# The conditioning sums of a two-layer hybrid transformer kernel, all moved beside the attention heads, with a written order for TensorE

## The chip, the cores and the metric

The kernel runs on one core of a Trainium2 chip. The metric is the time of one execution on the device in microseconds (us). TensorE (PE) multiplies, VectorE (DVE), ScalarE (ACT) and GpSimd (POOL) do the elementwise work, and SyncE (SP) issues nearly all transfers from HBM.

## The reference, cut to what matters

One sequence of 512 tokens of width 1024 (and 256 context tokens) passes two layers. Layer 0 mixes with differential attention (6 heads, each with two score maps) and a Fourier branch, layer 1 with a short convolution. Each mixer is followed by a mixture of 16 experts. Six conditioning vectors per layer shift, scale and gate all this.

```python
sh_m, sc_m, g_m, sh_f, sc_f, g_f = split(silu(c) @ ada_w[l] + ada_b[l], 6)   # 1024 x 6144, each layer
s = einsum('bqhmd,bkhmd->bhmqk', q, k)                 # m = 0, 1; 512 queries, 768 keys
p = softmax(s)
a = p[:, :, 0] - lam * p[:, :, 1]
att = rmsnorm(einsum('bhqk,bkhe->bqhe', a, v), subln) * (1 - lam_init)
x = x + g_m * (concat(att, fourier) @ w_out)           # layer 0; in layer 1 the convolution
x = x + g_f * ec_moe(modulate(x, norm_ffn, sh_f, sc_f), ...)
```

## The kernel before, in words

The program is traced in Python. A scheduler then orders each engine's instructions by their place in the program (a smaller number goes first) as its own cost model finds them ready; on the chip each engine works through that fixed list and waits at semaphores. So an instruction whose input is late stops everything behind it on its engine.

The execution has four stages: attention (`attention`, to about 431 us in the profile), the experts of layer 0 (`moe`), the convolution (`conv`, about 915 to 1125 us), and the experts of layer 1.

Attention goes head by head, and each head in four steps `i` of 128 queries. While head `h` is attended to, the projections of head `H = h + 1` run as well: `proj` does one of six tiles of 128 tokens, 8 x 3 matmuls of 384 columns (256 for the two context tiles), because most operands are split into a high and a low part (`split`, `mm3`: three single-pass matmuls stand for one of full precision). `proj_fin` norms and rotates a tile on ACT, DVE and POOL, and `proj_tr` transposes two tiles of q and k. `scores` fills the PSUM tiles s0 and s1, `maxexp` takes the maxima on DVE and the exponentials on ACT, `normalise` combines the two maps, `att_tr` transposes the result in two groups of three, each into one of the two PSUM banks `tr` and out of it again, and `values` multiplies by v for two steps at once. `subnorm` and `subscale` norm what comes out. `fourier` runs behind heads 0 and 1. In the last head there is no projection left, and `wo.fill` begins the output projection.

The conditioning vectors are summed beside this by `ada_steps`: each is four parts of 1 MB (`ada_part`: a transfer, one ACT scaling, two DVE multiply-adds of 512 columns, and for all but the first part two POOL additions into `acc`, of which there is one buffer), and then `ada_sum` brings `acc` across the partitions on PE. Of the ten vectors that are not needed at once, seven are spread over 21 steps of the attention and three (`range(LW, 6)`, layer 1) over 11 steps of the convolution. Their parts share a ring of four 1 MB slots with the weights (wqk, wv, the Fourier matrix dft, later wo and cw); the transfers are issued in order by SP.

Line numbers in profiles: L68 is any `mm`, L251 and L250 the DVE and the ACT half of `split`, L174 and L176 the multiply-adds and additions of `ada_part`, L466 and L467 `maxexp`, L473 to L476 `normalise`, L489 `att_tr`, L443 `proj_tr`, L154 a load. Tiles: al and ah are the halves of the transposed attention, qv a head's values, ones<-ada the matmuls of `ada_sum` (an fp32 matmul of full precision is two instructions in the trace).

## Time and profile before

| | |
|---|---|
| time before, median of 3 runs | 1606.08 us (1604.41 to 1611.53) |
| the profiled execution | 1609.78 us, of which the span from first to last instruction is 1608.0 us |
| busy share of the span | PE 94%, DVE 42%, ACT 24%, POOL 14% |
| read from HBM | 491.41 MB |

A group of rows below is one view of this profiled execution. A busy PE includes the modelled tail of each matmul, so the distance from one start to the next is the better price of a matmul in a stream.

### The profile page before, as it was taken

The numbers are of one execution on the slowest core, as the hardware profiler recorded it, in microseconds if no ns is written. First come the engines' busy times: TensorE is split into PE (matmuls) and PEld (weight loads), VectorE is DVE, ScalarE is ACT, GpSimd is POOL, SyncE is SP. The second block draws the span as 40 slices with busy tenths as digits, with TensorE's granted clock in tenths as the row PEclk, the third lists the DMA queues.
The fourth block names the chain that finished last, engine by engine and source line by source line (L and its number), as shares of the span: only waits on it lengthen the run. The fifth ranks groups of instructions, "written<-read, shape, count | busy, mean of one in ns | idle before, by whom it ended". The sixth has DMA issues, their size and how long they took to land. (4 is left out here: it accounts for less than half of the span.)

```text
span 1608.0 us, 19864 instructions
## 1 busy us (share of the span) xinstructions
PE 1517.4 (94%) x7936; PEld 898.3 (56%) x7936; DVE 677.1 (42%) x1336; ACT 388.0 (24%) x753; POOL 225.3 (14%) x234
## 2 busy tenths in 40 slices
PE   4989999888999999999999899999899999999997
PEld 2978888777544444444443487887444444444443
DVE  3868788897612122112212567463312221221222
ACT  4535565553111001000100444232110010010000
POOL 0334355553000000000000024311000000000000
PEclk9889999999999999999999999999999999999999
DMA  9533444462799999999999766437999999999997
GB/s 346 168 103 106 156 136 155 158 236 104 302 364 360 410 409 409 409 409 409 409 409 404 265 209 209 157 131 271 348 399 399 409 409 409 410 408 409 409 409 278
DMA packets 162778, 494.79 MB, mean 308 GB/s; under 512 B 11750, under 2 KB 42879, under 8 KB 161663
## 3 DMA queue, kind: packets, MB, share of 16 engines
q1 hardware_dynamic: 161600, 491.23, 79.9%
q10 hardware_dynamic: 1086, 2.31, 0.4%
q8 instruction: 62, 1.02, 0.3%
q14 instruction: 30, 0.24, 0.0%
HBM read 491.41 MB, written 2.10 MB: 307 GB/s over the span
## 5 line engine op out<-in xcount | busy, mean ns | idle before, releaser
L1005 PE MATMUL s<-we,xs 128*64 128x512 f32 x1024 | 230.3, 597 | 0.0
L1005 PE MATMUL pj<-we,xs 128*64 128x512 f32 x1024 | 225.0, 593 | 4.5 <-DMA we<-in_moe_w_up_dram 4.5
L1005 PE MATMUL s<-we,aT 128*64 128x512 f32 x896 | 206.3, 603 | 0.0
L1005 PEld LDWEIGHTS pj<-we,xs 128*64 128x64 f32 x1024 | 75.6, 137 | 151.2 <-issue 140.8
L68 PEld LDWEIGHTS tr<-oh,x 128*128 128x128 f32 x1024 | 119.3, 191 | 50.2 <-issue 48.7
L1005 PEld LDWEIGHTS s<-we,xs 128*64 128x64 f32 x1024 | 69.3, 137 | 131.4 <-issue 125.8
L68 PE MATMUL tr<-oh,x 128*128 128x128 f32 x1024 | 131.2, 282 | 1.3 <-DVE oh L961 1.3
L1081 DVE TENSOR_TENSOR act<-act,pj 128x512 f32<-128x512 f32 x32 | 21.9, 688 | 261.3 <-PE pj L1005 240.3
L980 DVE TENSOR_SCALAR xs<-tr,am,ada 128x128 f32<-128x128 f32 x64 | 26.2, 409 | 230.4 <-PE tr L68 230.4
L1005 PEld LDWEIGHTS s<-we,aT 128*64 128x64 f32 x896 | 59.7, 137 | 103.2 <-issue 97.2
L1030 DVE TENSOR_TENSOR x<-x,tr 128x512 f32<-128x512 f32 x64 | 43.7, 685 | 139.8 <-PE tr L68 139.8
L176 POOL TENSOR_TENSOR ada<-ada,adaw 128x512 f32<-128x512 f32 x60 | 87.5, 1471 | 92.5 <-DVE adaw L174 45.4
L978 ACT ACTIVATE xs<-tr,ada,am 128x128 f32<-128x128 f32 x64 | 29.3, 458 | 273.2 <-DVE xs L980 273.2
L68 PE MATMUL pj<-whi,hh 128*128 128x384 f32 (+1 forms) x256 | 85.6, 334 | 0.3 <-ACT whi L250 0.3
L68 PE MATMUL pj<-wlo,hh 128*128 128x384 f32 (+1 forms) x256 | 83.1, 325 | 0.0
L68 PE MATMUL pj<-whi,hl 128*128 128x384 f32 (+1 forms) x256 | 83.0, 324 | 0.0
L1189 POOL TENSOR_TENSOR crs<-xsq 128x4 f32<-128x4 f32 x1 | 0.2, 203 | 485.2 <-ACT xT L1156 485.2
L1075 ACT ACTIVATE act<-s 128x512 f32<-128x512 f32 x32 | 17.4, 594 | 201.9 <-PE s L1005 168.3
L68 PE MATMUL pj<-chh,chi 128*128 128x512 f32 x160 | 62.4, 390 | 0.0
L68 PE MATMUL pj<-chl,chi 128*128 128x512 f32 x160 | 62.1, 389 | 0.0
L68 PE MATMUL pj<-chh,clo 128*128 128x512 f32 x160 | 62.0, 389 | 0.0
L710 POOL TENSOR_TENSOR wol<-wg,woh 128x512 fp32r<-128x512 f32 x32 | 47.2, 1489 | 96.6 <-ACT woh L709 91.7
(325 smaller groups left out, 2417.3 us busy)
## 6 DMA issues: line engine op xcount, KB each, us to landing
we<-in_moe_w_gate_dram SPq DMA_DIRECT2D x128, 1024.0 KB, 18.1
we<-in_moe_w_up_dram SPq DMA_DIRECT2D x128, 1024.0 KB, 18.2
we<-in_moe_w_down_dram SPq DMA_DIRECT2D x124, 1024.0 KB, 17.2
adaw<-in_ada_w_dram SPq DMA_DIRECT2D x48, 1024.0 KB, 5.6
cw<-in_conv_w_in_dram SPq DMA_DIRECT2D x12, 1024.0 KB, 6.4
wqk<-in_attn_w_in_dram SPq DMA_DIRECT2D x10, 512.0 KB
wo<-in_attn_w_out_dram SPq DMA_DIRECT2D x4, 1024.0 KB
we<-in_moe_w_down_dram SPq DMA_DIRECT2D x8, 512.0 KB
```

Source lines behind the costliest of these rows:

```text
L68: return T.matmul(o, l, r, start=start, stop=stop, skip_group_check=True)
L176: G.tensor_tensor(acc[:, cs], acc[:, cs], o, op=ALU.add)
L710: G.tensor_tensor(lo, wg, hi.bitcast(F32), op=ALU.subtract)
L978: A.activation(o_, i_, AF.Identity, bias=sh[:, kk:kk + 1], scale=am[:, kk:kk + 1])
L980: V.tensor_scalar(o_, i_, am[:, kk:kk + 1], sh[:, kk:kk + 1], op0=ALU.mult, op1=ALU.add)
L1005: pe(T.matmul(acc[hf][64 * j:64 * j + 64, :], lhs[:, 2 * kk + k, 64 * j:64 * j + 64], ws[j][:, k, hf * 512:hf * 512 + 512], start=kk == 0 ...
L1030: V.tensor_tensor(x1[tt][:, cs], src[tt][:, cs], b, op=ALU.add)
L1075: A.activation(act[:, hf * 512:hf * 512 + 512], ga[hf], AF.Silu)
L1081: V.tensor_tensor(act[:, cs], act[:, cs], up[hf], op=ALU.mult)
L1189: G.tensor_tensor(rs, xsq[:, :, 0], xsq[:, :, 1], op=ALU.add)
```

## The change: what it does

- `mm`, `turn` and the two matmuls of `subscale` are chained: in heads 0 to 4 each of them may be placed on PE only behind the one traced before it. The loop is rewritten: within a step come an even projection tile, `values` (now a step later), the next scores, `subnorm`, an odd projection tile, the rest of `fourier`, `subscale`, `proj_tr` and `att_tr`. `ada_sum`, the gate rows and the last head aren't in the chain.
- All ten vectors are summed in 20 steps of the attention, two parts a step; `conv` has none. `ada_sum` is traced at the start of the step behind a vector's last part, and is 4 packed matmuls of 256 columns, an ACT copy and 2 transposes in place of 8 matmuls of one column.
- v and the transposed attention are no longer split: `values` is 6 full-precision matmuls in place of 18 single-pass ones, and the ACT half of the split alone remains.
- `normalise` scales one map only (one ACT scaling of 768 columns less); the other map's sum goes into the epsilon of the norm behind it.
- A column is spread over a tile by one transpose (`spread`) in place of a matmul with the identity.
- The rotated sine table is half as large, and its multiplication is two DVE instructions in place of one.

```diff
+    def spread(o, col):
+        return T.transpose(o, col.to_broadcast([128, 128]), ident)
...
+    order = {"on": False, "last": None}
+    def inorder(m):
+        if order["on"]:
+            if order["last"] is not None:
+                tc.add_manual_dep(m.ins, order["last"].ins.name, NOSYNC, reason="the order of the heads")
+            order["last"] = m
+        return m
...
-        return T.matmul(o, l, r, start=start, stop=stop, skip_group_check=True)
+        return inorder(T.matmul(o, l, r, start=start, stop=stop, skip_group_check=True))
+    def turn(o, i):
+        return inorder(T.transpose(o, i, ident))
...
-        for k in range(KD):
-            mm(b[:, k:k + 1], acc[:, k * 128:k * 128 + 128], one1, True, True)
-        V.tensor_tensor(adaT[l, 0][:, w, :], b[:, :KD], biasT[:, l, w, :], op=ALU.add)
+        for q in range(4):
+            T.matmul(b[32 * q:32 * q + 32, 0:256], one1.to_broadcast([128, 32]), acc[:, 256 * q:256 * q + 256],
+                     start=True, stop=True, skip_group_check=True, tile_position=(0, 32 * q))
+        A.copy(acc[:, 0:256], b[:, 0:256])
+        for c in range(2):
+            T.transpose(b[:, 256 + c * 128:384 + c * 128], acc[:, c * 128:c * 128 + 128], ident)
+        V.tensor_tensor(adaT[l, 0][:, w, :].rearrange("p (q c) -> p c q", c=2),
+                        b[:, 256:512].rearrange("p (c q r) -> p c q r", c=2, q=4)[:, :, :, 0],
+                        biasT[:, l, w, :].rearrange("p (q c) -> p c q", c=2), op=ALU.add)
...
-            while n < len(todo) and n * steps < (step + 1) * len(todo):
+            if acc is not None and n % 4 == 0:
+                ada_sum(*todo[n - 1][:2], acc)
+                acc = None
+            while n < len(todo) and n * steps < (step + 1) * len(todo) and (acc is None or n % 4):
...
-                    if acc is not None:
-                        ada_sum(*todo[n - 2][:2], acc)
...
-                m = mm(b[:, k * 128:k * 128 + 128],
-                       adaT[l, 0][:, 2 + 3 * which, 4 * q + k:4 * q + k + 1].to_broadcast([128, 128]), ident,
-                       True, True)
+                m = spread(b[:, k * 128:k * 128 + 128], adaT[l, 0][:, 2 + 3 * which, 4 * q + k:4 * q + k + 1])
...
-        sing = tabs.tile([128, NT, 2, 2, 64], F32, name="sing")
+        sing = tabs.tile([128, NT, 2, 64], F32, name="sing")
...
-                for m in range(2):
-                    V.tensor_tensor(sing[:, :, j, m, :], sing[:, :, 1, 1, :],
-                                    gx_[:, j, None, :].to_broadcast([128, NT, 64]), op=ALU.mult)
+                for b in range(4):
+                    V.tensor_tensor(sing[:, :, j, 16 * b:16 * b + 16], sing[:, :, 1, 16 * b:16 * b + 16],
+                                    gj[:, None, 16 * (b ^ 1):16 * (b ^ 1) + 16].to_broadcast([128, NT, 16]),
+                                    op=ALU.mult)
...
-            a, b = [qkv.tile([128, 2048], F32R, tag="w", name=n) for n in ("qk", "qv")]
-            QKV[h] = ([a[:, 1536:], b[:, 1536:]], [a[:, :768], a[:, 768:1536]],
-                      [b[:, i:i + 768].rearrange("p (i d) -> p i d", i=6) for i in (0, 768)], {})
+            a = qkv.tile([128, 2048], F32R, tag="w", name="qk")
+            b = slot("qv", qkv)
+            ql = ap_.tile([128, S], F32R, tag="ql", name="ql", bufs=2)
+            QKV[h] = ([a[:, 1536:], ql], [a[:, :768], a[:, 768:1536]],
+                      b[:, :768].rearrange("p (i d) -> p i d", i=6), {})
...
-            split(v[0][:, tt, :], v[1][:, tt, :], p[:, 256:384])
+            A.copy(v[:, tt, :], p[:, 256:384])
...
-                src = p[:, :256].rearrange("p (g b i) -> p g b i", b=2, i=16)
-                V.tensor_tensor(t2.rearrange("p (g b i) -> p g b i", b=2, i=16), src[:, :, ::-1, :],
-                                sing[:, tt].rearrange("p j m (u b i) -> p (j m u) b i", u=2, b=2), op=ALU.mult)
+                for j in range(2):
+                    js = slice(128 * j, 128 * j + 128)
+                    V.tensor_tensor(t2[:, js].rearrange("p (m u b i) -> p m u b i", m=2, u=2, b=2),
+                                    p[:, js].rearrange("p (m u b i) -> p m u b i", m=2, u=2, b=2)[:, :, :, ::-1, :],
+                                    sing[:, tt, j, None, :].to_broadcast([128, 2, 64]).rearrange(
+                                        "p m (u b i) -> p m u b i", u=2, b=2), op=ALU.mult)
...
+        def normalise(i, p, su):
+
+            if i % 2 == 0:
+                AT["e"] = sm.tile([128, 2], F32, tag="e2", name="e2")
+            A.activation(AT["e"][:, i % 2:i % 2 + 1], su[:, 0:1], AF.Square, scale=EPS ** 0.5)
             rc = sm.tile([128, 2], F32, tag="rc", name="rc")
-            V.reciprocal(rc, su)
-            V.tensor_tensor(rc[:, 1:2], rc[:, 1:2], lam, op=ALU.mult)
-            A.activation(p[:, 1, :], p[:, 1, :], AF.Copy, scale=rc[:, 1:2])
-            V.scalar_tensor_tensor(p[:, 0, :], p[:, 0, :], rc[:, 0:1], p[:, 1, :], op0=ALU.mult,
-                                   op1=ALU.subtract)
-
-        AT = {}
+            V.reciprocal(rc[:, 0:1], su[:, 1:2])
+            V.scalar_tensor_tensor(rc[:, 1:2], su[:, 0:1], rc[:, 0:1], nlam, op0=ALU.mult, op1=ALU.mult)
+            V.scalar_tensor_tensor(p[:, 0, :], p[:, 1, :], rc[:, 1:2], p[:, 0, :], op0=ALU.mult, op1=ALU.add)
...
-                AT[0] = [ap_.tile([128, 6, 256], F32R, tag=f"a{x}", name=f"a{x}") for x in "hl"]
-            ah, al = AT[0]
+                AT[0] = ap_.tile([128, 6, 256], F32, tag="a" + "hl"[i // 2], name="at")
...
-                    T.transpose(b[:, c * 128:(c + 1) * 128], p[:, 0, (i0 + c) * 128:(i0 + c + 1) * 128],
-                                ident)
-                split(ah[:, i0:i0 + 3, qs], al[:, i0:i0 + 3, qs],
-                      b[:, :384].rearrange("p (i q) -> p i q", i=3))
...
+                    turn(b[:, c * 128:(c + 1) * 128], p[:, 0, (i0 + c) * 128:(i0 + c + 1) * 128])
+                A.copy(AT[0][:, i0:i0 + 3, qs], b[:, :384].rearrange("p (i q) -> p i q", i=3))
...
-                mm3(o[:, :256], (v[0][:, i, :], v[1][:, i, :]), (ah[:, i, :], al[:, i, :]), i == 0, i == 5)
+                mm(o[:, :256], v[:, i, :], a[:, i, :], i == 0, i == 5)
...
-            V.tensor_scalar(r, b[:, 256:258], 1.0 / 128, EPS, op0=ALU.mult, op1=ALU.add)
+            V.scalar_tensor_tensor(r, b[:, 256:258], 1.0 / 128, e2, op0=ALU.mult, op1=ALU.add)
...
-                mm(b[:, i * 128:i * 128 + 128], r[:, i:i + 1].to_broadcast([128, 128]), ident, True, True)
+                inorder(spread(b[:, i * 128:i * 128 + 128], r[:, i:i + 1]))
...
-            p = bank("pj", None)
-            for i in range(2):
-                mm(p, fh["bd"][i], fs[i], i == 0, i == 1)
-            V.tensor_copy(oT[:, 6 + g, :], p)
...
+            def rest():
+                p = bank("pj", None)
+                for i in range(2):
+                    mm(p, fh["bd"][i], fs[i], i == 0, i == 1)
+                V.tensor_copy(oT[:, 6 + g, :], p)
...
+            return rest
...
             H = h + 1 if h + 1 < NH else None
             for i in range(4):
                 p, su = maxexp(s)
+                if H and i < 3:
+                    proj(H, 2 * i)
+                if due:
+                    pend = values(*due)
+                    due = None
+                if i < 3:
+                    s = scores(h, i + 1)
+                normalise(i, p, su)
                 if pend:
                     pend = subnorm(*pend)
                 if H and i < 3:
-                    proj(H, 2 * i)
-                if i < 3:
-                    s = scores(h, i + 1)
-                normalise(p, su)
-                if H and 0 < i:
-                    proj_tr(H, i - 1)
+                    proj(H, 2 * i + 1)
+                if rest:
+                    rest = rest()
                 if pend:
                     subscale(*pend)
                     pend = None
+                if H and 0 < i:
+                    proj_tr(H, i - 1)
                 att_tr(h, i, p)
+                if i % 2:
+                    due = h, i // 2, AT[0], AT["e"]
                 if H and i == 3:
                     s = scores(H, 0)
-                if H and i < 3:
-                    proj(H, 2 * i + 1)
-                if i % 2:
-                    pend = values(h, i // 2)
                 if not H:
+                    if due:
+                        pend = values(*due)
+                        due = None
                     wo.fill(i, fold_router)
-                    fourier(h)
+                    rest = fourier(h)
...
-            mm(rb[:, tt * 128:tt * 128 + 128], rs[:, tt:tt + 1].to_broadcast([128, 128]), ident, True, True)
+            spread(rb[:, tt * 128:tt * 128 + 128], rs[:, tt:tt + 1])
...
-NSTEP = 21
-LW = 3
+NSTEP = 20
+LW = 6
```

## Rows read from the trace of the kernel before

**Rows 1.** The page's 40 slices (40.2 us each): granted PE clock in tenths, GB/s moved.

```profile
PEclk9889999999999999999999999999999999999999
GB/s 346 168 103 106 156 136 155 158 236 104 302 364 360 410 409 409 409 409 409 409 409 404 265 209 209 157 131 271 348 399 399 409 409 409 410 408 409 409 409 278
```

**Rows 2.** Windows, heads 0 to 5: length; busy PE, PEld, DVE, ACT, POOL; clock, DMA, GB/s.

```profile
93.03:135.42 42.39, 40.96 (x264) 35.92 (x265) 31.92 (x71) 24.68 (x57) 13.48 (x21) 0.97 0.15 51
135.42:187.35 51.93, 49.44 (x327) 43.47 (x327) 39.46 (x83) 25.85 (x54) 24.03 (x28) 0.97 0.39 126
187.35:240.13 52.78, 49.49 (x327) 43.75 (x327) 45.08 (x96) 33.60 (x70) 25.33 (x28) 0.97 0.52 176
240.13:287.96 47.83, 43.45 (x297) 37.86 (x296) 40.20 (x85) 27.63 (x61) 25.14 (x28) 1.00 0.40 132
287.96:342.36 54.40, 46.33 (x314) 41.12 (x312) 49.35 (x89) 30.18 (x61) 33.98 (x32) 0.94 0.63 218
342.36:389.43 47.07, 40.89 (x228) 33.41 (x228) 37.58 (x54) 19.76 (x37) 20.21 (x15) 0.96 0.37 134
```

**Rows 3.** PE's own waits from 90 to 395 us: total, times, longest.

```profile
PE tr L489 <- DVE p L476: 6.1, 6, 1.6
PE tr L68 <- DVE al L251: 5.8, 5, 3.3
```

**Rows 4.** Timeline of PE in head 0: start, us, what (x runs of one kind).

```profile
128.66 1.99 PE L68 MATMUL pj<-dft,oT 128*128 128x256 f32 x8
130.49 0.49 PE L489 MATMUL tr<-ident,p 128*128 128x128 f32 x3
...
135.21 0.39 PE L68 MATMUL tr<-ah,qv 128*128 128x256 f32 x1
...
137.42 1.02 PE L68 MATMUL pj<-four,bd_c 128*128 128x512 f32 x2
```

**Rows 5.** Timeline of PE beside the convolution, at two of the three sums.

```profile
965.42 1.84 PE L68 MATMUL tr<-ones,ada 128*128 128x1 f32 x16
967.12 0.48 PE L68 MATMUL pj<-chh,chi 128*128 128x512 f32 x1
...
992.25 2.79 PE L68 MATMUL tr<-ones,ada 128*128 128x1 f32 x16 [1.33 <-ACT gate L225]
```

**Rows 6.** Timeline of PE: four matmuls of 32 columns packed beside each other.

```profile
1119.71 0.85 PE L816 MATMUL tr<-xT,ra 128*32 128x384 f32 x8
1120.49 0.66 PE L831 MATMUL s<-ident,x 128*128 128x128 f32 x4
```

**Rows 7.** DVE groups, 93-342.4 us: count | busy, mean ns; L174's min/median/max ns, 90-400.

```profile
L174 DVE SCALAR_TENSOR_TENSOR adaw<-adaw,cin 128x512 f32<-128x512 f32 x35 | 30.3, 886 | 2.4 <-ACT adaw L170 2.4
L251 DVE TENSOR_TENSOR al<-tr,ah 128x384 fp32r<-128x384 f32 x40 | 21.7, 551 | 2.2 <-ACT ah L250 2.0
...
L251 DVE TENSOR_TENSOR qv<-pj,qv 128x128 fp32r<-128x128 f32 x30 | 8.4, 282 | 0.8 <-ACT qv L250 0.8
...
L174 DVE SCALAR_TENSOR_TENSOR adaw<-adaw,cin x39: 725/744/1796, 89.9 to 352.1; 128x512 f32<-128x512 f32 x39
```

**Rows 8.** Windows in and before the convolution (columns as in rows 2).

```profile
990.00:1000.00 10.00, 8.65 (x36) 6.88 (x35) 7.39 (x11) 7.04 (x12) 4.49 (x3) 0.66 0.72 219
1085.00:1100.00 15.00, 15.00 (x70) 12.93 (x69) 3.00 (x6) 0.62 (x1) 0.00 (x0) 0.77 0.67 237
```

**Rows 9.** Timeline of SP: start, us over which the loads were issued, count.

```profile
96.97 64.56 SPq L154 DMA_DIRECT2D adaw<-in_ada_w_dram  x6
...
273.53 34.30 SPq L154 DMA_DIRECT2D adaw<-in_ada_w_dram  x6
```

**Rows 10.** Timelines of PE and of DVE: the transposes of one `proj_tr`, the copy that ends it.

```profile
173.35 0.66 PE L443 MATMUL tr<-ident,qk 128*128 128x128 f32 x4
...
176.93 0.42 DVE L251 TENSOR_TENSOR qk<-tr,qk 128x256 fp32r<-128x256 f32 x1
```

**Rows 11.** Window just after the transposes that open the convolution (columns as in rows 2).

```profile
920.00:925.00 5.00, 5.00 (x13) 3.88 (x13) 5.00 (x9) 2.51 (x4) 0.00 (x0) 0.52 0.21 84
```

More of the change, by code (lines that the diff above doesn't have):

```diff
@@ L115, in body @@
     subg = cst.tile([128, 1], F32, name="subg")
-    lam = cst.tile([128, 1], F32, name="lam")
+    nlam = cst.tile([128, 1], F32, name="nlam")
     def small_loads(st):
@@ L144, in small_params @@
         A.activation(le, pl[:, 0:2], AF.Exp)
[L145 removed]
+        V.scalar_tensor_tensor(nlam, le[:, 1:2], LAM0, le[:, 0:1], op0=ALU.subtract, op1=ALU.subtract)
     def slot(name, pl=None):
@@ L201, in ada_steps @@
             yield
-        ada_sum(*todo[-1][:2], acc)
+        while n < len(todo) or acc is not None:
+            if acc is not None and n % 4 == 0:
+                ada_sum(*todo[n - 1][:2], acc)
+                acc = None
+                continue
+            l, w, j = todo[n]
+            n += 1
+            if j == 0:
+                acc = new()
+            ada_part((l, w, acc), j)
         yield
@@ L304, in attention @@
         cosg = tabs.tile([128, NT, 2, 64], F32, name="cosg")
-        sing = tabs.tile([128, NT, 2, 2, 64], F32, name="sing")
+        sing = tabs.tile([128, NT, 2, 64], F32, name="sing")
         gk1 = tabs.tile([128, 64], F32, name="gk1")
-        gx_ = tabs.tile([128, 2, 64], F32, name="gx")
         def table_loads(st):
@@ L321, in tables @@
             V.tensor_scalar(gb[:, 0, :], gb[:, 0, :], 0.125, None, op0=ALU.mult)
-            for b in range(4):
-                V.tensor_copy(gx_[:, :, 16 * b:16 * b + 16], gb[:, :, 16 * (b ^ 1):16 * (b ^ 1) + 16])
             for j in range(2):
@@ L442, in proj_tr @@
                     if j or g < 2:
-                        T.transpose(b[:, j * 256 + i * 128:j * 256 + i * 128 + 128],
-                                    nat[2 * g + i][:, j, :], ident)
+                        turn(b[:, j * 256 + i * 128:j * 256 + i * 128 + 128], nat[2 * g + i][:, j, :])
             cc = slice(g * 256, g * 256 + 256)
@@ L488, in att_tr, with values @@
                 for c in range(3):
-                    T.transpose(b[:, c * 128:(c + 1) * 128], p[:, 0, (i0 + c) * 128:(i0 + c + 1) * 128],
-                                ident)
-                split(ah[:, i0:i0 + 3, qs], al[:, i0:i0 + 3, qs],
-                      b[:, :384].rearrange("p (i q) -> p i q", i=3))
-        def values(h, qp):
+                    turn(b[:, c * 128:(c + 1) * 128], p[:, 0, (i0 + c) * 128:(i0 + c + 1) * 128])
+                A.copy(AT[0][:, i0:i0 + 3, qs], b[:, :384].rearrange("p (i q) -> p i q", i=3))
+        def values(h, qp, a, e2):
             v = QKV[h][2]
-            ah, al = AT[0]
             o = bank("tr", None)
             for i in range(6):
-                mm3(o[:, :256], (v[0][:, i, :], v[1][:, i, :]), (ah[:, i, :], al[:, i, :]), i == 0, i == 5)
+                mm(o[:, :256], v[:, i, :], a[:, i, :], i == 0, i == 5)
             sq = sm.tile([128, 256], F32, tag="osq", name="osq", bufs=1)
@@ L503, in values, with subnorm @@
             V.tensor_copy(at, o[:, :256])
-            return at, sq, h, qp
-        def subnorm(at, sq, h, qp):
+            return at, sq, e2, h, qp
+        def subnorm(at, sq, e2, h, qp):
             b = bank("tr", None)
@@ L619, in attention @@
                         NSTEP, lambda: sm.tile([128, D], F32, tag="ada", name="ada", bufs=1))
-        pend = None
-        wo = None
+        pend = due = rest = wo = None
         for h in range(NH):
             H = h + 1 if h + 1 < NH else None
+            order["on"] = H is not None
             if H:
@@ L895, in route @@
         bc = bank("tr", None)
-        n = spread(bc, isel, 0)[1]
+        n = tokens(bc, isel, 0)[1]
         gs = tmp.tile([NE, 2, CAP], F32, name="gs")
@@ L910, in route, with tokens @@
         return gf, bc
-    def spread(b, isel, e):
+    def tokens(b, isel, e):
         return [mm(b[:, j * CAP:j * CAP + CAP], ident[:NE, e + j:e + j + 1].to_broadcast([NE, 128]),
@@ L956, in onehot @@
                 b = bank("tr", None)
-                for m in spread(b, isel, e):
+                for m in tokens(b, isel, e):
                     pe(m)
```

5 lines of the change are left out of this document (2 added, 3 removed).

## The prediction

> **What bounds the kernel now.** I read the page's slices first. In both expert stages the transfers stand flat at about 409 GB/s, and they do so from the end of the stage before [rows 1]: those stages end a fixed time after their stream of weights can start. So a microsecond won in the attention or beside the convolution is won at the end, and one won among the experts is not. The change touches just those two stages, where the transfers run at a third to a half of that rate.
>
> Next, the attention head by head [rows 2]. Heads 0 to 4 take 249.3 us (93.0 to 342.4). PE is busy for 229.7 us of it, so it idles for 19.7. The granted clock falls short of full speed by 0.03, 0.03, 0.03, 0 and 0.06 of the five lengths: 7.8 us. What is left, about 222 us, is matmul work. DVE is busy for 206 us, 83%. PE sets the end, DVE is close behind, and the reader should see how little idle time there is to win. The waits say where it lies: PE stood about 1 us each time for DVE's combining of the maps or for DVE to empty a PSUM bank [rows 3]. Head 5 takes 47.1 us with 6.2 idle.
>
> Beside the convolution PE runs almost without a gap, so work taken off PE counts there in full. Three groups of one-column matmuls stand in it (two are shown, the third, at 1086, is like the first) [rows 5], and in the stretches around two of them the clock is at 0.66 and 0.77 [rows 8].
>
> **The change part by part: heads 0 to 4.**
>
> *Values.* Before, 18 single-pass matmuls in 137.42 - 135.21 = 2.21 us; full-precision matmuls of the same 256 columns start (130.49 - 128.66)/8 = 0.229 us apart [rows 4]. The new 12 instructions cost 2.75 us, 0.54 more. Nine pairs of steps fall into these heads: +4.9 us. What is saved is DVE's: the low halves al (21.7 us) and of v (8.4 us) [rows 7].
>
> *Sums.* One is 16 instructions in 967.12 - 965.42 = 1.70 us [rows 5]. The trace has no sum of the new kind. Eight packed instructions of 384 columns take 1120.49 - 1119.71 = 0.78 us [rows 6]; with 256 columns that bounds them from above if they run beside each other; one after the other, at 0.229, they would take 1.8. I take 0.78, since these too are 32 columns wide, plus 0.12 for two transposes (three of them fit into 0.33 us, 130.49 to the dft matmul after it, an estimate): 0.9. Six old sums save 0.8 each, three more come: -4.8 + 2.7 = -2.1 us (with 1.8: +6).
>
> *Spreading.* Each matmul with the identity is two instructions, each transpose one; at 1.70/16 = 0.106 us, nine times two in `subscale` and eight in the gate row save 26 x 0.106 = -2.8 us.
>
> So PE's own work stays as it is: 4.9 - 2.1 - 2.8 = 0.
>
> *Clock.* The dips stand behind stretches of many small matmuls. With the one-column groups gone I count half of the 7.8 us back: -4 (0 to -7.8).
>
> *The other engines.* DVE loses 30.1 us [rows 7]. The conditioning parts that run in these heads grow from 23 or 24 to some 37 of the 40, which is 27 more multiply-adds at 0.744: +20. The split rotation adds some 3, so DVE drops to about 199 us. ACT loses twenty scalings of 768 columns and gains thirteen of 1024 and ten small copies, near nothing; POOL gains some twenty additions. None becomes the bound of a stretch of 240 us; what hides them is PE's 222 us, and if a head were to fall under 40 us DVE would be next.
>
> *Idle time.* This is the real unknown. The written order gives each product a projection tile of PE work as cover: the maxima and exponentials of a step run under `proj`, the norm under the odd tile. But `subscale`, `proj_tr` and `att_tr` come in a row, with two `tr` banks for four users. The second group of `att_tr` can't begin before ACT and DVE have emptied the bank of `proj_tr`, and in a chain nothing else may fill the gap; before, the scheduler put projection matmuls there. Behind PE's instruction the whole chain queues, the next scores and maxima too. Fifteen steps of heads 0 to 4 have this. At best the copies take under a microsecond, mostly covered: 0.6 each, 9 in all. In the row nearest to it the transposes begin at 173.35 and the last copy ends at 177.35 [rows 10]; less the half microsecond that PE needs itself, 3.5 each, and 5 for the rest: 57. I take 1.2 each, by PE's present waits of about a microsecond for DVE [rows 3] since DVE has less to do: 18, which is -1.7 against 19.7.
>
> Heads 0 to 4: 0 - 4 - 1.7 = about -6 us.
>
> DVE's multiply-adds take 744 ns at the median and up to 1796, with a mean of 886 [rows 7]: some are held up. The Trainium skill (SBUF — State Buffer, section SBUF: two separate sides) says that a DVE instruction with two SBUF inputs and a GpSimd one that reads SBUF exclude each other for their whole length. By that rule, with which the spread agrees, some twenty more POOL additions would hold DVE up at just the steps where PE now waits for it, and with 0.6 us more a step the sum would end 9 us worse.
>
> **Head 5 and what follows.** DVE's low halves are gone there too. PE's longest single wait for one (3.3 us) was here [rows 3]; I count half of the 6.2 us of idle time: -3 (0 to -5).
>
> **Beside the convolution.** Three sums go: 1.70 twice and 2.7 us [rows 5], 6.1. Twelve spreads become transposes: 12 x 0.106 = 1.3. The clock costs 0.34 x 10 + 0.23 x 15 = 6.9 us in the two stretches [rows 8], about 1 of which is in the cold sum already. In both, two groups of small matmuls followed each other, and one of the two goes; behind the sum at 965.42 alone the clock stayed up. I count half of the rest: 3 (0 to 6). Twelve transfers of 1 MB leave the ring, and twelve parts leave ACT, DVE and POOL, where PE hides them anyway: nothing. Sum: -10.4 (-7 to -14).
>
> **The total.** -6 - 3 - 10.4 = -19.4 us. Made against the profiled execution, 1609.8, that gives 1590.4. That execution is 3.7 above the median of the runs, so the forecast for the median is 1606.1 - 19.4 = 1586.7: 1587 us.
>
> **The rivals.**
>
> *The heads close up.* The order does what it could: 9 us idle, the clock held (-4 more), the conditioning beside it hidden. Then -9 and -4 in the heads, -3 more beside the convolution: 1571 us. For it: every product has a tile of cover. Against: the bank argument above.
>
> *The chain is too strict.* The wait behind `proj_tr` is that of rows 10, so 57 us of idle time: +37 where I count -2, and the total is 1587 + 39 = 1626 us. It eats the whole gain once a step waits about 2.5 us, and shows as slower from about 3. For it: DVE is busy 83% of the time, and its list is in program order, so the rotation of the odd tile comes ahead of the copies. Against: 30 us of DVE work leaves exactly there.
>
> *The conditioning stream sets the end of attention.* In head 0 the ring is nearly blocked by weights and the Fourier matrix: six loads were issued over 64.6 us from 96.97 on; later six in 34.3, 5.7 us each [rows 9]. If twelve of the 40 parts are done when the second head ends, at about 187 us, the other 28 need 160 us, until 347, some 13 us behind the end of head 4 that I expect (93 + 243 = 336, less a little for the last sum). The output weights queue behind them on SP: 1600 us, no change worth the name. Against: PE, DVE and ACT waited little for these loads so far.
>
> *Transposes let the clock fall.* Ahead of the convolution, after a stretch of transposes and waits, PE ran at 0.52 for 5 us [rows 11], 2.4 us lost. The gate rows that come in the middle of each routing become transposes, eight in place of sixteen instructions, and the experts' first matmuls follow at once. Two such dips would give 5 us back: 1592 us. The Trainium skill (TensorE: Matmul & The Clock Gate, section Part 4: PE-mode transpose) states that transposes don't count as activity for the clock; the row agrees without proving it, as PE also waited there.
>
> **How the numbers follow.** Half a per cent (8 us, about what a measurement of this kernel can tell from no change) sets the bounds at 1598 and 1614. Forecast 0.46 (its own range 1576 to 1597), heads close up 0.17, transposes 0.08, stream 0.16 (0.03 of it faster), too strict 0.13 (0.02 of it within the bounds). Faster 0.74, same 0.15, slower 0.11. For eight in ten I go from the first rival's side, 1566, to just over no change, 1606.
>
> **What would show it.** Right: `values` at 12 instructions in about 2.7 us; sums of about 0.9 us on PE and none beside the convolution, with a full clock around 990 and 1090 of the old time; heads of 46 to 49 us; waits of about a microsecond behind `proj_tr`. Wrong: waits there of 2.5 us and more, or PE or DVE standing for conditioning loads; an expert stage that lengthens; or heads of 44 us.

## The result, and the profile after

The changed kernel takes 1622.32 us (median of six runs, 1614.96 to 1627.61) where the kernel before takes 1605.71: a ratio of 1.0103, 95% interval 1.0084 to 1.0123. It is slower by about 1%; the forecast was 1587, and the range ended at 1606. The profiled span grew from 1608.0 to 1625.8 us; the profiled execution of the changed kernel is the slowest of its six, some 5 us above the median.

By windows, heads 0 to 5 of the changed kernel (columns as in [rows 2]), then heads 0 to 4 as a whole, and head 5 with all that follows up to the routing (the choice of the experts):

```profile
90.56:132.90 42.34, 38.71 (x251) 33.54 (x251) 27.18 (x62) 19.52 (x52) 15.50 (x22) 0.94 0.22 73
132.90:195.54 62.64, 53.40 (x303) 44.62 (x303) 41.05 (x82) 28.50 (x64) 31.04 (x32) 0.88 0.39 135
195.54:257.67 62.13, 53.14 (x312) 44.95 (x313) 47.55 (x90) 32.78 (x74) 29.87 (x32) 0.93 0.58 193
257.67:314.04 56.37, 46.11 (x276) 38.82 (x275) 44.61 (x83) 28.98 (x65) 30.85 (x32) 0.88 0.49 169
314.04:371.83 57.79, 48.13 (x301) 40.98 (x300) 48.60 (x82) 31.67 (x65) 33.87 (x35) 0.94 0.71 245
371.83:417.52 45.69, 40.60 (x198) 31.26 (x198) 32.94 (x47) 17.23 (x37) 19.45 (x15) 0.89 0.46 160
...
90.56:371.83 281.27, 239.50 (x1438) 202.91 (x1438) 208.98 (x394) 141.46 (x320) 141.13 (x153) 0.91 0.49 168
371.83:464.30 92.47, 83.94 (x409) 62.76 (x410) 59.66 (x98) 29.92 (x64) 27.78 (x25) 0.91 0.51 184
```

The same last stretch in the kernel before:

```profile
342.36:431.00 88.64, 80.34 (x441) 62.10 (x442) 65.05 (x105) 31.51 (x61) 27.80 (x23) 0.98 0.48 177
```

Against [rows 2] the first head is as long as it was; the next four, in which the conditioning parts run, are longer. The five take 281.3 us in place of 249.3. PE idles for 41.8 us of that (19.7 before), and by the count used in the prediction (what the clock falls short of full speed, times the length) the clock costs 24.6 (7.7, where the prediction says 7.8). The two overlap, since the clock is low in part of the idle time too: 281.3 less both is 215, where the work is some 222. DVE was not relieved: 209 us busy, 206 before, 199 forecast.

Beside the convolution, from the first spread of its norm to the routing, the same view of the kernel before and of the changed one:

```profile
915.80:1126.90 211.10, 207.00 (x934) 167.57 (x934) 122.96 (x193) 72.30 (x117) 52.26 (x38) 0.95 0.56 194
```

```profile
952.10:1143.60 191.50, 190.14 (x874) 154.04 (x874) 101.29 (x165) 59.02 (x105) 23.95 (x20) 1.00 0.42 148
```

That is 19.6 us less, with a full clock to the end (0.66 and 0.77 in [rows 8]). So the balance of the span is -2.5 ahead of head 0 (90.56 for 93.03), +31.9 in heads 0 to 4, +3.8 from head 5 to the routing (92.5 for 88.6), +4.1 in the two expert stages (487.8 and 482.2 for 484.8 and 481.1) and -19.6 beside the convolution: together, but for rounding, the 17.8 seen.

The waits of PE, ACT and DVE from 90 to 345 us (total, times, longest), to be set beside [rows 3], which reach to 395 us:

```profile
PE tr L85 <- ACT at L525: 18.7, 13, 4.4
PE tr L69 <- POOL or L544: 4.5, 2, 2.9
PE tr L85 <- DVE oT L550: 3.1, 6, 1.8
...
ACT p L501 <- DVE nm L500: 32.6, 11, 5.1
ACT adaw L187 <- DMA adaw<-in_ada_w_dram: 19.4, 12, 5.0
...
DVE rc L513 <- ACT p L501: 19.9, 14, 3.6
```

PE stands before the second group of `att_tr` (L85) for ACT's copy (L525); ACT stands for the maxima of DVE. One such wait in the timelines of PE, ACT, DVE and POOL, in head 2:

```profile
231.83 0.60 PE L85 MATMUL tr<-ident,qk 128*128 128x128 f32 x4
232.26 0.49 PE L85 MATMUL tr<-ident,p 128*128 128x128 f32 x3
235.77 0.90 PE L85 MATMUL tr<-ident,p 128*128 128x128 f32 x3 [3.02 <-ACT at L525]
...
230.52 0.90 ACT L501 ACTIVATE p<-s,nm 128x768 f32<-128x768 f32 x1 [3.56 <-DVE nm L500]
...
234.21 1.15 ACT L187 ACTIVATE adaw<-adaw,cin 128x1024 f32<-128x1024 f32 x1
235.26 0.46 ACT L525 COPY at<-tr 128x384 f32<-128x384 f32 x1
...
224.63 3.48 DVE L191 SCALAR_TENSOR_TENSOR adaw<-adaw,cin 128x512 f32<-128x512 f32 x2
...
229.54 1.81 DVE L500 TENSOR_REDUCE nm<-s 128x1 f32<-128x768 f32 x2
...
236.24 0.41 DVE L283 TENSOR_TENSOR ql<-tr,qk 128x256 fp32r<-128x256 f32 x1
...
225.94 7.43 POOL L193 TENSOR_TENSOR ada<-ada,adaw 128x512 f32<-128x512 f32 x5
```

Read it from the bottom. POOL adds without a pause until 233.37 (the first of its additions, outside the row shown, starts at 224.28). The two multiply-adds on DVE that begin beside it at 224.63 take 3.48 us where two take 1.49 at the median of [rows 7]. Behind them in DVE's list stand a tile's rotation and then the maxima, which begin at 229.54; so the exponentials begin late, ACT's list slips by the same amount, with a conditioning scaling (L187) ahead of the copy, and PE, whose next instruction needs the bank, stands for 3 us. In all of heads 0 to 4 PE stood 26.2 us, in 19 waits, for this copy.

### The profile page after: what moved, and what is told of

It reads as the page before. It is cut to its first block, busy times and chain, and to the rows that moved or that the text cites. A ratio compares the mean times of both kernels' runs of the same rounds, so it can differ in the third digit from the quotient of the medians.

```text
span 1625.8 us, 19404 instructions
## 1 busy us (share of the span) xinstructions
PE 1514.7 (93%) x7744; PEld 888.2 (55%) x7744; DVE 654.1 (40%) x1276; ACT 373.4 (23%) x763; POOL 216.8 (13%) x234
## 4 chain that ended last, share of the span: by engine, by line
PE 78%; DVE 7%; DMA 5%; ACT 4%; POOL 2%; issue 2%; SPq 1%; DVEq 0%; ACTq 0%; POOLq 0%
PE s L1049 26%; PE pj L82 18%; PE tr L82 13%; PE pj L1049 12%; PE s L82 4%; DMA adaw<-in_ada_w_dram 3%; DMA we<-in_moe_w_down_dram 2%; PE pj L1151 1%; DVE adaw L191 1%; ACT p L501 1%; PE tr L85 1%; POOL ada L193 1%; DVE act L1125 1%; PE tr L1035 1%; ACT adaw L187 1%
## 5 line engine op out<-in xcount | busy, mean ns | idle before, releaser
L82 PEld LDWEIGHTS tr<-oh,x 128*128 128x128 f32 x1024 | 124.3, 199 | 50.2 <-issue 48.7
L82 PE MATMUL tr<-oh,x 128*128 128x128 f32 x1024 | 136.1, 289 | 1.3 <-DVE oh L1005 1.3
L82 PE MATMUL pj<-whi,hh 128*128 128x384 f32 (+1 forms) x256 | 89.4, 349 | 1.2 <-ACT whi L282 1.2
L754 POOL TENSOR_TENSOR wol<-wg,woh 128x512 fp32r<-128x512 f32 x32 | 43.1, 1361 | 179.5 <-ACT woh L753 179.5
L191 DVE SCALAR_TENSOR_TENSOR adaw<-adaw,cin 128x512 f32<-128x512 f32 x60 | 58.7, 1009 | 8.8 <-ACT adaw L187 8.8
```

The lines of the kernel that those rows point to most:

```text
L82: return inorder(T.matmul(o, l, r, start=start, stop=stop, skip_group_check=True))
L191: V.scalar_tensor_tensor(o, s[:, 0, cs], cin[:, 0, j:j + 1], s[:, 1, cs], op0=ALU.mult, op1=ALU.add)
L754: G.tensor_tensor(lo, wg, hi.bitcast(F32), op=ALU.subtract)
```

## The experiments

Each kernel was timed against the kernel before. "Heads" is the length of heads 0 to 4 and "DVE" its busy time in them, both by windows of the one profiled execution; time and ratio are those of the runs (the kernel before had medians of 1604.5 to 1606.2 in the sets). "chained" and "free" both mean the new parts in the new loop. e5 and e9 leave out the additions and e6 the scaling, so their conditioning sums are incomplete; they serve for the timing alone.

| kernel | vectors in attention | order | additions on | heads | DVE | time, us | ratio (95%) |
|---|---|---|---|---|---|---|---|
| before | 7 | old | POOL | 249.3 | 206.0 | 1605.7 | |
| changed | 10 | chained | POOL | 281.3 | 209.0 | 1622.3 | 1.0103 (1.0084-1.0123) |
| e1 | 10 | free | POOL | 249.7 | 204.3 | 1597.3 | 0.9961 (0.9934-0.9987) |
| e2 | 7 | chained | POOL | 251.6 | 182.7 | 1613.9 | 1.0064 (1.0039-1.0088) |
| e3 | 7 | free | POOL | 241.4 | 180.0 | 1600.6 | 0.9977 (0.9956-0.9998) |
| e4 | 10 | old, old parts | POOL | 275.6 | 226.2 | 1619.1 | 1.0092 (1.0062-1.0122) |
| e5 | 10 | chained | none | 249.5 | 185.0 | 1588.5 | 0.9888 (0.9866-0.9910) |
| e6, no ACT scaling | 10 | chained | POOL | 268.1 | 209.8 | 1607.8 | 1.0012 (0.9994-1.0030) |
| e7 | 10 | matmuls chained | POOL | 270.3 | 203.6 | 1611.9 | 1.0037 (1.0020-1.0054) |
| e8, gate by matmuls | 10 | free | POOL | 249.4 | 204.1 | 1594.3 | 0.9921 (0.9901-0.9940) |
| e9 | 10 | chained | fills on POOL | 258.6 | 183.9 | 1605.1 | 1.0004 (0.9988-1.0019) |
| e10 | 10 | free | DVE | 247.7 | 210.8 | 1593.9 | 0.9928 (0.9905-0.9952) |
| e11 | 10 | free | half each | 251.4 | 215.7 | 1596.5 | 0.9950 (0.9934-0.9966) |
| e12 | 10 | old, new parts | POOL | 262.7 | 213.3 | 1600.9 | 0.9965 (0.9949-0.9982) |
| e13 | 10 | chained | DVE | 261.7 | 215.8 | 1599.5 | 0.9967 (0.9946-0.9987) |
| e14 | 10 | old, old parts | DVE | 273.0 | 228.7 | 1626.4 | 1.0120 (1.0100-1.0140) |
| e15 | 7 | old, old parts | DVE | 244.0 | 209.5 | 1589.9 | 0.9889 (0.9869-0.9908) |
| e16 | 7 | free | DVE | 223.4 | 184.1 | 1577.4 | 0.9828 (0.9796-0.9860) |
| e17 | 8 | free | DVE | 232.4 | 193.1 | 1577.2 | 0.9822 (0.9790-0.9854) |
| e18 | 9 | free | DVE | 228.9 | 204.5 | 1571.2 | 0.9791 (0.9749-0.9832) |

### Chain or conditioning: e1 to e4

```diff
-            order["on"] = H is not None        # e1, e3
+            order["on"] = False
...
-NSTEP = 20                                     # e2, e3; e4 is the kernel before with 20 and 6
-LW = 6
+NSTEP = 21
+LW = 3
```

> The changed kernel with nothing chained: the new order of tracing stays, but the scheduler may place any matmul. Theory A (the chain is too strict: PE stands behind a transpose whose bank isn't empty yet): heads 0 to 4 fall from 281 to about 250 us, idle time of PE there from 42 to about 20, the whole about 1594 us (1588 to 1602). Theory B (thirteen more conditioning parts load DVE, ACT and POOL, and whoever sets PE's order waits for them): heads still 270 or more, the whole 1612 to 1624 us.

> The changed kernel with three vectors summed beside the convolution again, seven in 21 steps of the attention; the chain stays. Theory A: the heads hardly shorten (275 or more of 281 us) and the convolution is some 15 us longer, the whole 1630 to 1642 us. Theory B: heads of about 255 us, the convolution about 200, the whole 1604 to 1612 us.

> Both undone: nothing chained, three vectors beside the convolution; what is left are the new sums, values, norms and the new loop. Theory A: heads as without the chain alone, about 250 us or a little less, the whole 1600 to 1612. Theory B: heads about 250, as with the three vectors back alone, the whole 1600 to 1612; the two theories part at the two kernels with one of them undone.

> The kernel before with all ten vectors in 20 steps of the attention and none beside the convolution, in its own loop, with its own sums of eight one-column matmuls. Theory A: the heads take some 5 us more than before (255), the convolution some 15 us less, the whole about 1595 us (1588 to 1602). Theory B: the heads take 270 or more, the whole 1610 to 1622 us.

Heads 0 to 4 by windows, in e1, e2, e3 and e4:

```profile
90.97:340.70 249.73, 226.54 (x1435) 188.89 (x1436) 204.29 (x393) 139.52 (x320) 141.38 (x152) 0.99 0.54 187
```

```profile
90.42:341.99 251.57, 222.93 (x1409) 191.60 (x1409) 182.71 (x367) 130.13 (x308) 113.38 (x136) 0.97 0.41 142
```

```profile
90.51:331.89 241.38, 226.16 (x1404) 192.45 (x1405) 179.99 (x366) 129.29 (x307) 114.15 (x136) 0.95 0.43 146
```

```profile
89.87:365.51 275.64, 246.42 (x1553) 215.40 (x1553) 226.15 (x441) 151.23 (x307) 149.87 (x155) 0.92 0.52 179
```

Neither theory holds alone. e1 came as A said, with the heads at 249.7. But e2, with the chain in place, came as B said for the heads (251.6; its time, 1613.9, is 2 us above B's range), and e4, which has no chain at all, as B said too (275.6). In e3 the heads are shorter (241.4) than either had. The thirteen parts cost the heads 29.7 us where chained (281.3 - 251.6), 26.3 in the old loop (275.6 - 249.3) and 8.3 free (249.7 - 241.4); the chain costs 10.2 with seven vectors and 31.6 with ten. Each cost grows with the other. The reading that fits is that the chain makes PE wait for delays that the conditioning makes on other engines: e1 has the same parts, and DVE is nearly as busy (204 us), at heads of 249.7. The sizes are those of single executions, of the changed kernel its slowest and of e2 its fastest; by the medians the chain costs 13.3 us with seven vectors (1613.9 - 1600.6) and 25.0 with ten (1622.3 - 1597.3). The moved vectors also save more beside the convolution than was counted: in e4, with the old spreads, it takes 192.4 us where the kernel before takes 211.1.

### Which of a part's instructions: e5, e6, e9; where in the chain: e7

```diff
             if j:                                                            # e5: both lines go
-                G.tensor_tensor(acc[:, cs], acc[:, cs], o, op=ALU.add)
+                for _ in range(3):                                           # e9
+                    G.memset(o, 0.0)
...
-        A.activation(s[:, 1, :], s[:, 1, :], AF.Copy, scale=...)             # e6
...
-        return inorder(T.transpose(o, i, ident))                             # e7, subscale too
+        return T.transpose(o, i, ident)
```

> The changed kernel without GpSimd's additions of the conditioning parts (the later quarters of a vector are not added to the sum, so the conditioning is incomplete); loads, scalings and multiply-adds stay. Theory B1 (GpSimd's additions hold up VectorE's multiply-adds and all that is queued behind them): heads 0 to 4 fall from 281 to 265 us or less, and the mean multiply-add from 1032 to about 750 ns; the whole 1606 or less. Theory B2 (ScalarE's scalings, which stand waiting for their transfer in its queue, hold up the copies that PE waits for): heads 275 or more, the whole 1616 or more.

> The changed kernel without ScalarE's scaling in the conditioning parts (one half of each part goes unscaled into the sum); VectorE's multiply-add then waits for the transfer itself. Theory B2: PE's waits for ScalarE's copy of the transposed maps nearly vanish and heads 0 to 4 fall from 281 to 265 us or less, the whole 1606 or less. Theory B1: heads 275 or more, the whole 1616 or more. If each takes some 8 us, both engines count in the same chain.

> The changed kernel, chained, with each addition of GpSimd replaced by three fills of 512 columns of its own operand (the later quarters of a vector don't reach the sum): GpSimd waits for the same multiply-add, stays busy for about as long, but reads nothing from SBUF. Theory P (an addition and VectorE's multiply-adds shut each other out while both read SBUF): the multiply-add falls from 1032 to about 770 ns and heads 0 to 4 to about 252 us, as without additions; the whole 1588 to 1596. Theory Q (what hurts is GpSimd's queue: the norms' powers and the scaling of q and k stand behind the additions): heads 272 or more, the whole 1612 or more.

> The changed kernel with its transposes (projected tiles, combined maps, spread norms) out of the chain; the matmuls stay chained to one another, and all ten vectors stay in the attention. Theory A1 (PE stands because the next matmul may not pass a transpose that waits for its bank): heads 0 to 4 fall from 281 to about 253 us, as without any chain, the whole about 1600 (1594 to 1605). Theory A2 (the order of projection, values and scores among themselves binds): heads 270 or more, the whole 1612 or more.

Heads 0 to 4 by windows in e5 and in e9, then DVE's multiply-adds (count | busy, mean ns) in the changed kernel, in e5 and in e9, and their shortest, median and longest in the changed kernel and in e9:

```profile
85.65:335.12 249.47, 225.73 (x1431) 191.91 (x1432) 185.03 (x398) 142.62 (x323) 60.69 (x100) 0.95 0.58 199
```

```profile
88.75:347.31 258.56, 227.96 (x1433) 193.06 (x1434) 183.89 (x398) 141.95 (x322) 141.11 (x265) 0.95 0.55 190
```

```profile
L191 DVE SCALAR_TENSOR_TENSOR adaw<-adaw,cin 128x512 f32<-128x512 f32 x49 | 48.9, 1032 | 8.3 <-ACT adaw L187 8.3
```

```profile
L191 DVE SCALAR_TENSOR_TENSOR adaw<-adaw,cin 128x512 f32<-128x512 f32 x54 | 39.7, 766 | 15.8 <-ACT adaw L187 15.6
```

```profile
L191 DVE SCALAR_TENSOR_TENSOR adaw<-adaw,cin 128x512 f32<-128x512 f32 x54 | 39.2, 752 | 22.8 <-ACT adaw L187 22.7
```

```profile
L191 DVE SCALAR_TENSOR_TENSOR adaw<-adaw,cin x49: 734/747/1781, 89.2 to 342.1; 128x512 f32<-128x512 f32 x49
```

```profile
L191 DVE SCALAR_TENSOR_TENSOR adaw<-adaw,cin x54: 730/745/1101, 97.2 to 329.2; 128x512 f32<-128x512 f32 x54
```

Without POOL's additions the chained heads fall by the whole 31.8 us, although all loads, scalings, multiply-adds and sums are still there: B1. In e9 POOL is busy for the same 141 us, now with fills; the multiply-add is at 752 ns all the same, and the heads give back 22.7 us. So what slows the multiply-adds is not that POOL works, but that it reads SBUF beside them. The mean hides how: of the 72 multiply-adds in heads 0 to 4 of the changed kernel 13 took 1.75 to 1.78 us, about a microsecond more than the median, and most of the rest nothing more. The medians divide it more evenly: from 1622 to 1605 with fills and on to 1588 without them, so some 17 us each, and P's ranges for the heads (252) and the time (1588 to 1596) were missed. The second half, which fills cost too, I can't place: e9's profiled execution was its fastest, and the waits of e5 and e9 show no row of that size. Theory P for the larger part by the profile and for half by the medians, then, with a remainder that Q may own.

ACT's scalings cost 13.2 us in the same chain (e6, 268.1), which fits their place ahead of the copies; the bound of 265 for B2 was just missed. And e7, at 270.3 us and 1611.9, stands at the bounds of A2 (270 and 1612): that the matmuls are chained to each other costs more than that the transposes are, though with free transposes a third of the chain's cost goes.

### The gate rows: e8

e1, with `spread` in `gate_row` replaced by the matmul with the identity of the kernel before.

> The kernel without the chain, with the gate rows spread by matmuls with the identity as in the kernel before, in place of transposes. Theory G (after transposes alone the clock falls: 0.66 over 10 us in the second routing): the clock behind the gate rows stays at 1.0 there, each expert stage ends 1 to 2 us earlier, the whole 2 to 4 us below the kernel without the chain (1597), that is 1593 to 1595. Theory H (the dip comes from the waits of that stretch, or the stream of weights covers it): the same time within 1 us, with the same dip in the first case.

The second routing in the timeline of PE, the gate row and the experts' gathers behind it, and the window around the gathers: the kernel before, then e8.

```profile
1135.10 2.02 PE L68 MATMUL tr<-ident,ada 128*128 128x128 f32 x16 [0.45 <-DVE tv L876]
...
1141.06 4.03 PE L68 MATMUL tr<-oh,x 128*128 128x128 f32 x32 [0.67 <-DVE oh L961]
```

```profile
1141.90:1146.90 5.00, 5.00 (x38) 3.71 (x38) 1.18 (x3) 0.92 (x2) 0.00 (x0) 1.00 0.67 261
```

```profile
1121.38 2.02 PE L82 MATMUL tr<-ident,ada 128*128 128x128 f32 x16 [0.46 <-DVE tv L922]
...
1127.33 6.75 PE L82 MATMUL tr<-oh,x 128*128 128x128 f32 x32 [0.67 <-DVE oh L1007]
```

```profile
1128.20:1133.20 5.00, 5.00 (x25) 5.00 (x25) 0.74 (x2) 0.46 (x1) 0.00 (x0) 0.50 0.65 260
```

The same instructions with the same waits ran at full clock in one kernel and at 0.50, which is the lower level, in the other. So the dip doesn't need the gate row's transposes, as H said; but the waits, to which H put it, don't account for it either, as the kernel before has them without the dip. (The run's median, 1594.3, is G's time, 3 us below e1's; but they were timed in different sets, the intervals of the ratios overlap, and e8's profiled span is the longer one.)

### Additions on DVE: e10, e11, e13 to e15; the old loop: e12

```diff
-                G.tensor_tensor(acc[:, cs], acc[:, cs], o, op=ALU.add)
+                V.tensor_tensor(acc[:, cs], acc[:, cs], o, op=ALU.add)       # e11: for one of two
```

e10 and e11 are e1 with this, e13 the changed kernel, e14 is e4, e15 the kernel before. e12 is e1 with the order of the old loop.

> The kernel without the chain, with all additions of the conditioning parts on VectorE in place of GpSimd. Some 56 additions more on VectorE at some 0.6 us (an estimate from its multiply-adds of the same size) are 33 us, against 13 us that its multiply-adds save when GpSimd is silent. Theory P: VectorE 204 + 20 = 224 us of 250, heads unchanged within 4 us of 250, the whole 1594 to 1602. Theory R (VectorE's own load is what binds): heads 258 or more, the whole 1604 or more.

> The kernel without the chain, with one of each two additions on VectorE, the other on GpSimd. Theory P: half of the exclusion goes for some 17 us more on VectorE: heads 244 to 250, the whole 1590 to 1598. Theory R: heads 253 or more, the whole 1600 or more.

> The changed kernel's parts (unsplit values, packed sums, the shorter norm, all ten vectors in the attention), nothing chained, in the loop order of the kernel before. Theory S (the new loop, with values a step later, makes the stream of conditioning cheap where the old loop pays 26 us for it): heads 265 or more, the whole 1608 or more. Theory T (the new parts make it cheap, above all less work on VectorE): heads about 250 as in the new loop without the chain, the whole 1593 to 1601.

> The changed kernel, chained, with all additions of the conditioning parts on VectorE, none on GpSimd; nothing is left out. VectorE gets some 56 additions at 0.685 us (38 us) and its multiply-adds fall from 1032 to about 750 ns (-14). Theory P (what the chain stands behind is the trouble that GpSimd's additions make: exclusion and GpSimd's queue): heads 0 to 4 fall from 281 to 262 us or less, the whole 1594 to 1605. Theory R (in a chain any more work on VectorE or ScalarE ahead of the copies is paid): VectorE at 233 us and more, heads 272 or more, the whole 1613 or more.

> The kernel before with all ten vectors in the attention, in its own loop, and the additions on VectorE. With the additions on GpSimd its heads took 275.6 us, with VectorE busy for 226. Theory P: heads 264 or less, the whole 1608 or less, though VectorE rises to about 245. Theory R (VectorE is the engine that binds in the old loop with ten vectors): heads 275 or more, the whole 1617 or more.

> The kernel before, with seven vectors in the attention and three beside the convolution, with all additions on VectorE. Theory P: with fewer parts there is less trouble to remove, heads 244 to 250 of 249 us, the whole 1598 to 1605. Theory R: VectorE goes from 206 to about 228 us of 249, heads 255 or more, the whole 1610 or more.

Heads 0 to 4 in e13, and DVE's groups:

```profile
85.12:346.85 261.73, 232.22 (x1427) 194.81 (x1426) 215.79 (x455) 142.44 (x322) 64.46 (x99) 0.92 0.53 184
```

```profile
L191 DVE SCALAR_TENSOR_TENSOR adaw<-adaw,cin 128x512 f32<-128x512 f32 x54 | 39.6, 764 | 7.1 <-ACT adaw L187 7.1
L193 DVE TENSOR_TENSOR ada<-ada,adaw 128x512 f32<-128x512 f32 x55 | 35.8, 683 | 0.0
```

e13 is the changed kernel with nothing left out and 36 us of additions put onto DVE. DVE's busy time rises by only 7, the heads fall by 19.6 us, and 1622 becomes 1599: theory P for the chain. The kernel before gains 1.1% by the same line alone (e15), more than P had. The heads are not all of it: of e15's 16.6 us of span 5.4 lie in them, 7.1 ahead of head 0 (which begins at 86.0 in place of 93.0) and 5.9 beside the convolution. But in the old loop with ten vectors the line gains nothing (e14, 1626.4 us; e4 took 1619.1, with intervals that overlap): DVE is busy for 229 of 273 us there, the low halves of v and of the maps among it, and head 5 with what follows takes 105.6 us as against 92.5 in e4. The time is R's; the heads, at 273.0, lie between P and R, just below R's bound. e10 came as P said, but its time isn't clear of e1's; e11, with half of the additions moved, has P's time and heads no shorter than with none or all (251.4), which neither theory had. e12 has heads between S and T and the upper end of T's time: of the 26 us of heads between e4 and e1 the new parts are worth 13 (275.6 to 262.7) and the new order, unchained, the other 13.

### How many vectors: e16 to e18

e10 with `LW` of 3, 4 and 5 (`NSTEP` 21, 21 and 20).

> The changed kernel's parts without the chain, additions on VectorE, three vectors beside the convolution and seven in 21 steps of the attention. Theory P (with GpSimd silent a part costs the heads little, so the move pays what the convolution saves, 14 to 18 us for three vectors): the convolution about 205 us, attention some 10 us shorter than with all ten (347), the whole 1596 to 1602, above the 1594 with all ten. Theory R (VectorE's load is what the last three vectors cost): the attention 15 us or more shorter, the whole 1582 to 1592.

> The same with two vectors beside the convolution, eight in 21 steps of the attention. Theory P: between 1594 and 1600 us, each vector moved saves about 2 us. Theory R: 1585 to 1592, below the kernel with all ten, since attention shortens by more than the 5 us that a vector costs beside the convolution.

> The same with one vector beside the convolution, nine in 20 steps of the attention. Theory P: about 1595 us. Theory R: 1588 to 1592 us.

Heads 0 to 4 in e16, in e18, and in e10:

```profile
84.44:307.87 223.43, 216.61 (x1398) 184.75 (x1398) 184.05 (x401) 127.00 (x306) 62.69 (x99) 0.99 0.45 156
```

```profile
85.04:313.89 228.85, 219.37 (x1418) 185.29 (x1418) 204.51 (x436) 135.53 (x317) 65.17 (x99) 0.99 0.55 190
```

```profile
85.86:333.60 247.74, 233.13 (x1420) 193.98 (x1420) 210.84 (x449) 139.22 (x318) 64.20 (x99) 0.95 0.55 192
```

All three lie below the times of both theories. R had the direction, but that DVE's load is what the last vectors cost isn't shown: each vector takes ACT's scalings, the sums on PE and 4 MB of transfers with it. With no additions on POOL the heads are at 223 to 232 us, 17 to 26 below the kernel before. Nine vectors are the best that was run: 1571 us, 2.1% faster than the kernel before, with the convolution at 193.2. e18's interval overlaps those of e16 and e17, so only the step to ten vectors, which lengthens the heads by 19 us, is plain. Why the tenth costs so much wasn't tried; DVE's share doesn't tell, as it was busy for 89% of e18's heads and 85% of e10's.

## Why the prediction was wrong

**The other engines: the step that failed.** Twenty-seven more multiply-adds on DVE and some twenty more additions on POOL (25 and 18 by the traces) were costed at nothing, hidden by PE's 222 us, because no engine's busy time reached the length of the heads. With the scalings, sums and transfers of their parts they cost 26 us in the old loop (e4) and 30 in the chain. The error was to ask whether an engine has time left over, where what counts is how late each result comes that PE waits for next: DVE and ACT work through lists, and 3.5 us of held-up multiply-adds hold back the maxima, the exponentials and the copies behind them.

**The exclusion was seen and priced too low.** The prediction weighed what the Trainium skill (SBUF — State Buffer, section SBUF: two separate sides) states, that a DVE instruction with two SBUF inputs and a GpSimd one that reads SBUF exclude each other for their whole length, and said that the sum would end 9 us worse by it. By that rule fills, which read nothing, should leave the multiply-adds alone, and the trace agrees: 752 ns with fills and 766 without additions, against 1032. To take the additions off POOL gave 20 (e13) to 32 us (e5) of heads, POOL's queue included, and fills in their place 23 (e9). The bare delay of these multiply-adds is 49 x (1032 - 766) ns = 13 us; other DVE instructions were held as well, as all of DVE's busy time falls by 24 us in e5 (209.0 to 185.0) and 25 in e9. How much of the price is this delay itself and how much what stood behind it isn't shown.

**Idle time** was taken at 18 us and measured 41.8; the long waits are at the place named, ahead of the second group of `att_tr`, 3 us and more in the worst case. But the prediction had PE wait there for the bank of `proj_tr`; in the row shown the wait ends with the copy of the first group, while DVE still reads `proj_tr`'s bank at 236.24. **The clock** was to give 4 us back, as dips were put down to small matmuls, and cost 17 more, in stretches that follow such waits: in the 5 us up to 157.9 PE was busy for 1.82, and over the next 5 the clock was 0.79; in the 5 up to 272.6 for 2.07, and then the clock was 0.66. In e1 both come near the forecast: idle 23.2, and the clock, by the same count (0.05 of 41.3 us and 0.03 of 50.5), 3.6 us, so 4 us back as forecast. PE's own work came out as forecast there too: 249.7 - 23.2 - 3.6 = 222.9 us against about 222.

**The terms that held.** `values` take 211.39 - 208.71 = 2.68 us in the place of a forecast 2.75, and the eight packed instructions of a sum 0.64, less than the 0.78 taken:

```profile
208.71 2.75 PE L82 MATMUL tr<-at,qv 128*128 128x256 f32 x12
211.39 0.62 PE L82 MATMUL s<-qk 64*128 64x512 f32 x4
...
221.16 0.64 PE L199 MATMUL tr<-ada,ones 128*32 128x256 f32 x8
```

**Beside the convolution** the sign was right and the size too small: -19.6 for -10.4. The clock's term was mis-sized: it cost 0.05 of 211 us, about 10.5, all of which came back, where 3 were counted from two stretches alone. PE's idle time fell from 4.1 to 1.4 as well. The spreads are worth 0.9 (192.4 in e4 for 191.5) where 1.3 were counted; for the sums, at 6.1, no run has a number of its own.

**Head 5** and what follows were to save 3 us of idle time and cost 3.8 us more (2.3 in e1). The idle time stayed (8.5 for 8.3); by the same count the clock costs 0.09 of 92.5 us, 8.3, where it cost 1.8. No run took it apart.

**The rivals.** "The chain is too strict" forecast 1626 us and 57 us of idle time, from waits at the very place where they are; 1622 was measured, with 42 us idle and much of the rest in the clock. It was nearest, and its reason held only by half: the chain alone costs 10 us with seven vectors (e2 against e3), and 14 with ten and no additions on POOL (261.7 - 247.7). That conditioning loads set the end: no; e5 has the same loads, and its heads are as short as those of the kernel before. That transposes let the clock fall: the dip in the routing is there (0.66 over 10 us in the changed kernel, full clock before), but e8 has it with the gate row spread by matmuls. Of what the Trainium skill (TensorE: Matmul & The Clock Gate, Part 4: PE-mode transpose) states, that a transpose doesn't count as a busy TensorE in the same way, these runs show nothing for or against.

## What to carry to other kernels

Work that an engine has time for isn't hidden if it stands, in that engine's list, ahead of something that the bounding engine waits for next: cost it by the delay of that result, and ask again wherever a written order or a longer list leaves the bounding engine nothing else to do. GpSimd arithmetic on SBUF is not free help for a busy DVE: here the same additions cost less on DVE itself in the chain (e13) and in the kernel before (e15), and no gain was clear in the free order (e10) or in the old loop with ten vectors (e14), where DVE was busy for 229 of 273 us. When a change couples a new order with moved work, try each alone before judging either: here the order without its chain, with nine of the ten vectors moved and the additions on DVE, made 1571 us out of a change that had made 1622.

## What the runs showed of the hardware that was not expected

The granted clock behind the same instructions, with waits within 0.01 us of each other in the rows shown, was 1.00 in the kernel before and 0.50 in e8, and the gathers behind it took 4.03 and 6.75 us. PE's instructions are alike in both over the 14 us ahead of the gathers, with waits within 0.02 us; what decides the clock there these runs don't show. And `V.tensor_tensor` of 128x512 fp32, both inputs in SBUF, took 0.683 us on DVE (e13), where GpSimd took a median of 1.29 us for the same addition in the kernel before and 1.57 in the changed one (heads 0 to 4) and made the multiply-adds beside it slower by a third on average.
